# A decoder layer in split fp32 on one core: the weight ring moved by 32 bytes, GpSimd's additions given to VectorE, and two places for the modulation sums

## The chip, the core and the metric

The kernel runs on one core of a Trainium2 chip. A core has a matrix engine (TensorE, PE in the profile, with its weight loads as PEld), a vector engine (VectorE, DVE), a scalar engine (ScalarE, ACT), a general engine (GpSimd, POOL) and an engine that here only issues transfers (SyncE, SP). Each runs its own instructions in order. They share a memory on the chip of 128 partitions, in which addresses are counted in bytes of one partition. The metric is the time of one execution on the device in microseconds; lower is better.

## The reference

One layer of a decoder, 1024 tokens of width 1024, all in float32, cut to what is computed:

```python
mod = silu(cond) @ w_mod + b_mod
sh1, sc1, g1, sh2, sc2, g2, sh3, sc3, g3 = split(mod, 9)

h = rms_norm(x, ffn1_norm) * (1 + sc1) + sh1
x = x + 0.5 * g1 * ((silu(h @ w_gate1) * (h @ w_up1)) @ w_down1)      # FFN1, inner width 2816

h = rms_norm(x, mix_norm) * (1 + sc2) + sh2
b, c, v, u = split(h @ w_in, 4)                                       # each of width 512
yA = b * conv3_causal(c * v)
yB = gelu(Re(C . state) + D * u)       # state_t = Abar state_(t-1) + Bbar u_t, 32 groups of 64 states
yB = yB * sigmoid(yB @ glu_w + glu_b)
x = x + g2 * (concat(rms_norm(yA), rms_norm(yB)) @ w_out)

h = rms_norm(x, ffn2_norm) * (1 + sc3) + sh3
x = x + 0.5 * g3 * ((silu(h @ w_gate2) * (h @ w_up2)) @ w_down2)      # FFN2
return rms_norm(x, final_norm)
```

## The kernel before

**Stages.** In order of time: FFN1 (a prologue with the first norm, gate and up projections to 505 us, the down projection to about 720 us), the mixer's projections u, c, v and b with the eight batches of the state recurrence beside them, the GLU, the output projection `w_out` (about 985 to 1055 us), FFN2 (gate and up to about 1500 us, down to the end) and the last norm.

**Matmuls.** A float32 product is made of three passes (`mm3`, lines 324 to 326): the weight and the activation are each split into a high and a low part, and the passes are high by high, high by low and low by high, mostly with 128 weight columns and 512 moving columns. Both parts of a weight tile lie in one ring tile `w` of 8 KB a partition. ACT copies the high part into it (line 183), DVE subtracts it for the low part (line 184), from a raw tile of 8 KB that SP loads (`raw`). The ring has three buffers (`ringp`), a fourth in the middle of the kernel (`ring1b`), and, in the last down projection only, five more (`ring2`). A tile serves 24 matmuls of 512 columns in the feed-forward stages.

**Where the buffers lie.** Pools are stacked from the left or from the right end of a partition's memory. `ringp`, `rawp`, `tmp` (short-lived tiles) and `ring1b` stand on the right, above a block of constants whose last tile is a pad of `PAD[1]` columns of float32; `ring2`, the activations (`movA`) and others stand on the left, above a pad of `PAD[0]` columns. With 88 columns on the right the built program has the tiles of `ringp` at bytes 202720, 210912 and 219104 and that of `ring1b` at 165856, each 480 modulo 512. The five of `ring2` stand at 120320 to 153088, each 0 modulo 512.

**Feed-forward groups.** All but the first groups of gate and up, and both down projections, use seven products for eight (Strassen's scheme). It needs sums of weight blocks: `Weights.combine` (lines 151 to 153) makes them for gate and up from a raw tile, and `right_sums` (lines 602 to 605) for the down weights `wd`, which then go back to memory (line 612) until the down projection loads them. The sums of activations (`combos`, whose low parts line 336 makes, and `Left.sums`, lines 587 to 590) are DVE's.

**Who does what, and when.** A clock counts calls of `mm3`. Work can be put off by some ticks (`clock.after`), and generators in `clock.side` make one step every `clock.period` ticks. The tile framework then sets the order on each engine and the waits between engines. In FFN1 the weight sums run on DVE; in FFN2 `ws.adds` and an argument of `right_sums` put them on POOL. The sums of squares for the norms `n3` (before FFN2) and `n4` (the last) are accumulated by `Sumsq.add`: there `beside` sends the first five additions of each to POOL (line 353), the others run on DVE (line 355).

**Modulation.** Each of the nine modulation vectors takes eight sums over the condition (`mod_fetch`, line 447, loads 512 KB into a tile `wm`; `mod_next` multiplies and sums it on DVE, line 441). Those of G2, SC3 and SH3, 24 sums, are made by one generator `vectors` from the projection u on, one every 6 ticks. Beside them run the batches of the recurrence: a matmul group `px` (line 1297), a copy `X`, two transfers that swap halves (`swx`, `swz`, line 1287), products and scans on DVE (lines 1303 to 1314), and a matmul group `yy` (line 1324) that reads the result `co`. A loop behind the projections forces whatever of the sums is left (`while clock.side`).

The functions below also need these lines, which carry the last sums of squares of the mixer's norm: `roots` (lines 384 to 391) is a chain of twelve small DVE operations from the sums of squares to the reciprocal root.

Of the kernel before, what the change touches and what calls it, by code (L numbers as in the profile page):

```python
# [17 lines left out]
ALU = mybir.AluOpType  # L18
# [7 lines left out]
KT = D // P  # L26
# [17 lines left out]
GB = G // NB  # L44


PAD = 96, 88

C_BMOD, C_N1, C_N2, C_N3, C_NF, C_ONC, C_ONS, C_CW, C_GB = 0, 72, 80, 88, 96, 104, 108, 112, 124
NCOLS = 128  # L50
# [47 lines left out]
class Weights:  # L98
# [5 lines left out]
    SEVEN = (0, "t3", 1, 3, "t1", "t4", 2)  # L104

    def __init__(self, engines, srcs, granules, raw_bufs):
        self.V, self.A, self.SP, self.adds = engines
        self.srcs, self.granules, self.raw_bufs = srcs, granules, raw_bufs
        self.left = [0] * len(srcs)
        self.combined = {j for pair in granules for j, c in pair if isinstance(c, str)}  # L110
        for pair in granules:
            for j, _ in pair:
                self.left[j] += 1
        self.raws, self.tiles, self.sums, self.kinds = [], [], {}, []
        self.given = self.freed = 0
        self.sums_pool = None
        self.slots = deque()
# [27 lines left out]
    def combine(self, j):  # L145

        r = self.raws[j]
        t = self.sums_pool.tile([P, 3, HALF], F32, tag="sums", name=f"sums{j}")
        f = t[:].rearrange("p a b -> p (a b)")
        E = self.adds  # L150
        E.tensor_tensor(out=f[:, :1024], in0=r[:, 512:1536], in1=r[:, :1024], op=ALU.subtract)  # L151
        E.tensor_tensor(out=r[:, 512:1024], in0=f[:, 512:1024], in1=r[:, :512], op=ALU.add)
        E.tensor_tensor(out=f[:, 1024:], in0=r[:, 1536:], in1=r[:, 512:1024], op=ALU.subtract)
        self.sums[j] = {"t1": f[:, :512], "t3": f[:, 512:1024], "t4": f[:, 1024:]}

    def chunk(self, j, c):
# [55 lines left out]
def hymba_layer(ctx: ExitStack, tc, x_d, wm1_d, wmod_d, gu1_d, gs1_d, wd1_d, win_d, wout_d, glu_d, gu2_d, gs2_d, wd2_d, cols_d, cond_d, lam_d, bc_d, out_d):  # L212
    nc = tc.nc
    V, A, T, SP = nc.vector, nc.scalar, nc.tensor, nc.sync
# [4 lines left out]
    pad = pool("pad")  # L219
    pad.tile([P, PAD[0]], F32, name="pad_left")  # L220
    const = pool("const", side="right")
# [42 lines left out]
    srcs, granules = [], []  # L264
# [6 lines left out]
    t1_d, t2_d = (scratch.tile([4, KH, P, HALF], F32, name=f"t{n}_d")[:] for n in (1, 2))  # L271
# [25 lines left out]
    stream7(gu1_d, gs1_d, wd1_d, t1_d, SEVEN_FROM[0])  # L297
    plain([win_d[i] for i in range(8)] + [glu_d] + [wout_d[i] for i in range(4)])
    stream7(gu2_d, gs2_d, wd2_d, t2_d, SEVEN_FROM[1])
    ws = Weights((V, A, SP, V), srcs, granules, 2)  # L300
    ws.raw_pool = lambda i: rawp

    xt = [[None, None] for k in range(KT // 2)]
    x = [[None, None] for k in range(KT)]
# [8 lines left out]
    clock = Clock(4)  # L313
# [25 lines left out]
    class Sumsq:  # L339
# [3 lines left out]
            self.name, self.parts, self.n, self.home = name, [], n, home  # L343
            self.count = 0

        def add(self, src, apart=False, get=t2k, beside=False):
            nm, n = f"{self.name}q{self.count}", self.n
            sq = get(nm)[:] if self.parts else self.home(nm)
            A.activation(sq[:, :n], src, AF.Square)  # L349
            if self.parts and not apart:  # L350
                a = self.parts[0][:, :n]
                if beside:
                    nc.gpsimd.tensor_tensor(out=a, in0=a, in1=sq[:, :n], op=ALU.add)  # L353
                else:
                    V.tensor_tensor(out=a, in0=a, in1=sq[:, :n], op=ALU.add)
            else:
                self.parts.append(sq)
            self.count += 1
# [58 lines left out]
    def norm_into(act, h, ss, n, name, where="A", over=False):  # L417


        def use(bc):  # L420
            got = []
            for k in range(KT):
                clock.after(k, lambda k=k: got.append(modulated(k, h, bc, n, name, where, over)))
            act[h] = got

        ss.rstd(D, use, 8)
# [164 lines left out]
            self.store(2, 2, o[:])  # L591
            self.store(4, 2, e[:])

    def right_sums(k, wd_d, t_d, G_, where="A"):


        lo, hi = (mov(f"wd{k}_{i}", where, dtype=F32) for i in range(2))
        for i, t in enumerate((lo, hi)):
            SP.dma_start(t[:], wd_d[2 * i : 2 * i + 2, k].rearrange("c p n -> p c n"))
        b11, b12, b22, b21 = lo[:, 0, :], lo[:, 1, :], hi[:, 0, :], hi[:, 1, :]  # L600
        ops = [
            lambda: G_.tensor_tensor(out=b22, in0=b22, in1=b12, op=ALU.subtract),
            lambda: G_.tensor_tensor(out=b12, in0=b12, in1=b11, op=ALU.subtract),
            lambda: G_.tensor_tensor(out=b11, in0=b22, in1=b11, op=ALU.add),
            lambda: G_.tensor_tensor(out=b21, in0=b21, in1=b11, op=ALU.subtract),
        ]
        for i, op in enumerate(ops):
            clock.after(8 + 4 * i, op)

        def stores():  # L610
            for i, t in enumerate((lo, hi)):
                SP.dma_start(t_d[2 * i : 2 * i + 2, k].rearrange("c p n -> p c n"), t[:])

        clock.after(24, stores)
# [146 lines left out]
    for h in range(2):  # L761
        sqs = []
        for j in range(KT // 2):
            sq = pro.tile([P, 1024], F32, tag="sq", name=f"p{h}q{j}", bufs=3)
# [56 lines left out]
    left = Left(l1_d, 0, "fa0", "B")  # L821
# [287 lines left out]
    def vectors(count, where):  # L1109
        mod_fetch(where)  # L1110
        for i in range(count):
            mod_next()
            if i + 1 < count:
                mod_fetch(where)
            yield
# [41 lines left out]
    left = this  # L1157
    for g in range(SEVEN_FROM[0], NGRP):
        this = Left(l1_d, g, f"fa{g}", "B")
        hooks = {("g", 1): [left.sums], ("g", 5): [lambda g=g: right_sums(g - 2, wd1_d, t1_d, V, "B")]}  # L1160
        if g < 4:
            hooks["u", 5] = [lambda g=g: right_sums(g + 7, wd1_d, t1_d, V, "B")]
        if g == NGRP - 1:
            hooks["u", 2] = [lambda: lefts.load(2)]
            hooks["u", 5] = [lambda: lefts.load(4), lambda: lefts.ahead(3)]
        seven(f"fa{g}", this, hooks)
        left = this
# [67 lines left out]
    sp_open = ExitStack()  # L1235
    sp = sp_open.enter_context(tc.tile_pool(name="sp", bufs=1))
    clock.period = 6
    clock.side.append(vectors(3 * KT, "A"))
    w4 = ws.take(4)
    for h in range(2):  # L1240
        ready(act2, h, KT)
# [103 lines left out]
        ws.free()  # L1345
        v_tile(i, cs)

    while clock.side:
        clock.step()
    wb = ws.take(4)  # L1350

    def gate_b(i, h):
# [38 lines left out]
    n3 = [Sumsq(f"n3{c}", home=acc_in_mov) for c in "ab"]  # L1391
# [3 lines left out]
    def w_out(ds, h, part):  # L1395

        act = (actA, actB)[part]
        if part == 0:
            outs.update({(d, h): ps(f"wo{d}_{h}") for d in ds})
        for k in range(4):  # L1400
            ready(act, h, k + 1)
            for d in ds:
                mm3(outs[d, h][:], wo[d], 4 * part + k, act[h][k], part == k == 0, part == 1 and k == 3)
        if part == 0:
            return
        for d in ds:
            V.scalar_tensor_tensor(
                out=x[d][h], in0=outs.pop((d, h))[:], scalar=gate[:, 1, d : d + 1], in1=x[d][h], op0=ALU.mult, op1=ALU.add
            )
            n3[h].add(x[d][h], beside=d < 6)  # L1410
            if d % 2:
                SP.dma_start(x2_d[h, :, d - 1 : d + 1, :], xt[d // 2][h][:])

# [3 lines left out]
    w_out((0, 1), 0, 0)  # L1417
    glu(1)
    ws.free(2)
    wo.update(enumerate(ws.take(2), 2))  # L1420
    w_out((0, 1), 1, 0)
    w_out((0, 1), 0, 1)
# [10 lines left out]
    wo.update(enumerate(ws.take(4), 4))  # L1433
    w_out((4, 5, 6, 7), 0, 0)
    w_out((4, 5, 6, 7), 0, 1)
    norm_into(act3, 0, n3[0], 2, "h3", "B", True)
    ws.retire(ring1)
    for ds in ((4, 5), (6, 7)):
# [30 lines left out]
        ws.free()  # L1469
        return left  # L1470

    ws.adds = nc.gpsimd
    clock.period = 3
    clock.side.append(combos(act3, 2, "h3"))
    left = group0()
    lefts = Lefts(l2_d, "fbL")
    for g in range(1, NGRP):
        this = Left(l2_d, g, f"fb{g}")

        if 2 <= g:  # L1480
            mod_fetch("B")
            clock.after(40, lambda: fetched and mod_next())
        hooks = {("g", 1): [left.sums, lambda g=g: right_sums(g, wd2_d, t2_d, nc.gpsimd)]}
        if g == 4:
            hooks["u", 5] = [lambda: right_sums(0, wd2_d, t2_d, nc.gpsimd)]
        if g == NGRP - 1:
            hooks["g", 1].append(lambda: lefts.load(2))
            hooks["u", 5] = [lambda: lefts.load(4), lambda: lefts.ahead(3)]
        seven(f"fb{g}", this, hooks)
        left = this  # L1490
# [17 lines left out]
    def after2(d, h, done):  # L1508
        for tok in PIECES[h] if done == slice(0, HALF) else [done]:
            n = tok.stop - tok.start  # L1510
            if (h, tok.start) not in n4:
                n4[h, tok.start] = Sumsq(f"n4_{h}_{tok.start}", n, acc_in_mov)
            ss = n4[h, tok.start]
            ss.add(x[d][h][:, tok], apart=ss.count == KT - 1, beside=ss.count < 6)

            def use(bc, n=n, tok=tok):
                for k in range(KT):
                    xs = x[k][h][:, tok]
                    V.scalar_tensor_tensor(out=xs, in0=xs, scalar=cols[:, C_NF + k : C_NF + k + 1], in1=bc[:, :n], op0=ALU.mult, op1=ALU.mult)
                    if k % 2:  # L1520
                        SP.dma_start(out_d[h, :, k - 1 : k + 1, tok], xt[k // 2][h][:, :, tok])

            if ss.count == KT:
                ss.rstd(D, use)
# [70 lines left out]
```

## Time and profile before

| | |
|---|---|
| median of 3 runs | 1744.43 us (1743.91 to 1744.8) |
| the profiled execution | 1744.45 us, of which the span is 1742.5 |
| mean granted clock of TensorE | 0.992 |
| PE busy | 1685.0 us (97%), 7496 matmuls |
| DVE busy | 1212.8 us (70%) |
| ACT busy | 627.8 us (36%) |
| POOL busy | 217.1 us (12%), 135 instructions |

A page of the profile shows one execution. An engine's busy time is what its instructions took. "Idle before" is the time in which it stood, and the arrow names what ended that. In a list of instructions `w<-raw,w` means that tile `w` is written from `raw` and `w`; the numbers of tiles are left out. The table by stage cuts the span at times that I chose from where the tiles of a stage begin, and gives each engine's busy time within. Most of what follows is read from that table, from the list of who waited for whom, and from the instructions in order of time.

### The profile page before, as it was taken

The page shows a single profiled execution, that of the slowest core. Times are in us where ns is not written, and L with a number is a line of the kernel's source. Part 1 is how long each engine was busy: PE and PEld are TensorE (multiplying, and loading weights), DVE is VectorE, ACT ScalarE, POOL GpSimd, SP SyncE. Part 2 cuts the span into 40 slices and gives each one's busy share as a digit, 9 for nine tenths or more (in the row PEclk, how much of TensorE's full clock was granted, in tenths as well). Part 3 has the DMA queues.
Part 4 walks back from the last instruction along what each step waited for, and adds up shares of the span by engine and source line. Part 5 has one row for each costly group of instructions (what it writes and reads, how often), then busy time and mean ns, then how long its engine had stood idle before and what let it go on. Part 6 is the DMA issues. An engine that isn't in the chain of part 4 may idle for free.

```text
span 1742.5 us, 20320 instructions
## 1 busy us (share of the span) xinstructions
PE 1685.0 (97%) x7496; PEld 1358.3 (78%) x7496; DVE 1212.8 (70%) x2068; ACT 627.8 (36%) x957; POOL 217.1 (12%) x135
## 2 busy tenths in 40 slices
PE   4999999999999999999999999989999999999997
PEld 3788777777777888877888877867888888888887
DVE  7999876777778976847757639866566655557464
ACT  4333333333343434421115324523333333435340
POOL 0000000000000000000000021245453444101020
PEclk9999999999999999999999999999999999999998
DMA  7325765555588884668752211454443444667532
GB/s 304 122 71 176 246 233 191 177 183 170 170 297 295 312 297 163 220 196 261 224 151 67 73 73 51 138 199 167 179 167 145 163 162 174 242 237 257 209 126 97
DMA packets 149685, 321.81 MB, mean 185 GB/s; under 512 B 19793, under 2 KB 35409, under 8 KB 141266
## 3 DMA queue, kind: packets, MB, share of 16 engines
q1 hardware_dynamic: 149586, 320.53, 53.6%
q8 instruction: 58, 0.95, 0.2%
q14 instruction: 41, 0.34, 0.1%
HBM read 229.77 MB, written 86.51 MB: 182 GB/s over the span
## 4 chain that ended last, share of the span: by engine, by line
PE 85%; DVE 8%; DMA 4%; issue 1%; POOL 1%; ACT 1%; SPq 0%; DVEq 0%; ACTq 0%; POOLq 0%
PE fbDX L326 2%; PE fbDX L324 2%; PE fbDX L325 2%; PE faDX L324 2%; PE faDX L326 2%; PE faDX L325 2%; PE faDY L325 2%; PE faDY L326 2%; PE faDY L324 2%; PE fbDY L326 2%; PE fbDY L325 2%; PE fbDY L324 2%; PE wo L326 1%; PE wo L325 1%; PE wo L324 1%; DMA wm<-in_wmod 1%
## 5 line engine op out<-in xcount | busy, mean ns | idle before, releaser
L184 DVE TENSOR_TENSOR w<-raw,w 128x512 fp32r<-128x512 f32 (+1 forms) x268 | 267.2, 1003 | 157.5 <-ACT w L183 156.8
L183 ACT CAST w<-raw 128x512 fp32r<-128x512 f32 (+1 forms) x268 | 211.3, 803 | 291.0 <-PE faDX L326 59.4
L184 DVE TENSOR_TENSOR w<-sums,w 128x512 fp32r<-128x512 f32 x114 | 86.2, 770 | 85.3 <-ACT w L183 85.3
L353 POOL TENSOR_TENSOR n3aq<-n3aq,n3aq 128x512 f32<-128x512 f32 x5 | 6.5, 1291 | 1005.7 <-ACT n3aq L349 1005.5
L183 ACT CAST w<-sums 128x512 fp32r<-128x512 f32 x114 | 68.8, 620 | 77.4 <-POOL sums L151 4.7
L441 DVE CUSTOM_DVE_ANT_0 wm<-wm,cact 128x1024 f32<-128x1024 f32 x56 | 69.0, 1239 | 33.6 <-DMA wm<-in_wmod 33.4
L151 POOL TENSOR_TENSOR sums<-raw 128x1024 f32<-128x1024 f32 x20 | 54.8, 2739 | 192.9 <-DVE w L184 185.5
L326 PE MATMUL fbDX<-fbLh,w 128*128 128x512 f32 (+1 forms) x220 | 77.9, 354 | 0.0
L324 PE MATMUL fbDX<-fbLh,w 128*128 128x512 f32 (+1 forms) x220 | 77.8, 354 | 0.0
L325 PE MATMUL fbDX<-fbLl,w 128*128 128x512 f32 (+1 forms) x220 | 77.7, 353 | 0.0
L324 PE MATMUL faDX<-faLh,w 128*128 128x512 f32 x176 | 70.2, 403 | 2.1 <-ACT faLh L638 2.1
L325 PE MATMUL faDX<-faLl,w 128*128 128x512 f32 x176 | 70.0, 398 | 0.0
L326 PE MATMUL faDX<-faLh,w 128*128 128x512 f32 x176 | 69.9, 397 | 0.0
L639 DVE TENSOR_TENSOR fbLl<-fbLr,fbLh 128x1024 fp32r<-128x1024 f32 (+1 forms) x42 | 48.9, 1173 | 13.3 <-ACT fbLh L638 11.7
L325 PE MATMUL faDY<-faLl,w 128*128 128x512 f32 x132 | 52.2, 396 | 0.5 <-DVE faLl L639 0.5
L326 PE MATMUL faDY<-faLh,w 128*128 128x512 f32 x132 | 52.1, 395 | 0.0
L326 PE MATMUL fbDY<-fbLh,w 128*128 128x512 f32 x132 | 51.8, 393 | 0.0
L324 PE MATMUL fbDY<-fbLh,w 128*128 128x512 f32 x132 | 51.8, 393 | 0.0
L325 PE MATMUL fbDY<-fbLl,w 128*128 128x512 f32 x132 | 51.8, 393 | 0.0
L324 PE MATMUL faDY<-faLh,w 128*128 128x512 f32 x132 | 51.7, 395 | 0.0
L639 DVE TENSOR_TENSOR faLl<-faLr,faLh 128x1024 fp32r<-128x1024 f32 (+1 forms) x42 | 47.2, 1128 | 4.0 <-ACT faLh L638 4.0
L325 PEld LDWEIGHTS fbDX<-fbLl,w 128*128 128x128 f32 x220 | 42.5, 193 | 6.0
(2133 smaller groups left out, 4748.9 us busy)
## 6 DMA issues: line engine op xcount, KB each, us to landing
raw<-in_gs SPq DMA_DIRECT2D x38, 1024.0 KB, 5.5
wm<-in_wmod SPq DMA_DIRECT2D x56, 512.0 KB, 6.5
wd<-in_wd SPq DMA_DIRECT2D x44, 512.0 KB, 5.2
t_d<-wd SPq DMA_DIRECT2D x44, 512.0 KB, 3.5
faLr<-l_d SPq DMA_DIRECT2D x35, 512.0 KB, 8.1
fbLr<-l_d SPq DMA_DIRECT2D x35, 512.0 KB, 6.6
raw<-t_d SPq DMA_DIRECT2D x16, 1024.0 KB, 5.6
raw<-in_wd SPq DMA_DIRECT2D x12, 1024.0 KB, 5.6
```

Source lines behind the costliest of these rows:

```text
L151: E.tensor_tensor(out=f[:, :1024], in0=r[:, 512:1536], in1=r[:, :1024], op=ALU.subtract)
L183: self.A.copy(hi, src)
L184: self.V.tensor_tensor(out=lo, in0=src, in1=hi.bitcast(F32), op=ALU.subtract)
L324: T.matmul(out, lhsT=hi, rhs=ah, start=first, stop=False, skip_group_check=more)
L325: T.matmul(out, lhsT=hi, rhs=al, start=False, stop=False, skip_group_check=more)
L326: T.matmul(out, lhsT=lo, rhs=ah, start=False, stop=last, skip_group_check=more)
L353: nc.gpsimd.tensor_tensor(out=a, in0=a, in1=sq[:, :n], op=ALU.add)
L441: V.tensor_tensor_reduce(out=w, in0=w, in1=cact[:], scale=1.0, scalar=0.0, op0=ALU.mult, op1=ALU.add, accum_out=s)
L639: V.tensor_tensor(out=lo[:, :c, :], in0=src, in1=hi[:, :c, :].bitcast(F32), op=ALU.subtract)
```

## The change

Three edits:

1. `PAD` goes from `96, 88` to `96, 80`: the right-hand pad is eight columns (32 bytes) shorter, and all that stands to its left on that side moves by 32 bytes. In the built program `ringp`'s tiles then begin at 202752, 210944 and 219136 and `ring1b`'s at 165888, all 0 modulo 512; the raw tiles and the short-lived ones move in the same way. The left-hand pools stay.
2. POOL keeps only the set-up of constants. Its 129 additions go to DVE: the weight sums of FFN2's gate and up (20 sets of three), FFN2's right sums (44), and the ten additions of `n3` and fifteen of `n4`.
3. Of the 24 modulation sums, the eight of G2 stay where they were, and the sixteen of SC3 and SH3 are made from behind the second half of the GLU on, one every 4 ticks; the loop that forces the rest stands behind the output projection's first half for columns 4 to 7, ahead of the norm that uses them.

```diff
-PAD = 96, 88
+PAD = 96, 80
...
-        self.V, self.A, self.SP, self.adds = engines
+        self.V, self.A, self.SP = engines
...
-        E = self.adds
-        E.tensor_tensor(out=f[:, :1024], in0=r[:, 512:1536], in1=r[:, :1024], op=ALU.subtract)
-        E.tensor_tensor(out=r[:, 512:1024], in0=f[:, 512:1024], in1=r[:, :512], op=ALU.add)
-        E.tensor_tensor(out=f[:, 1024:], in0=r[:, 1536:], in1=r[:, 512:1024], op=ALU.subtract)
+        self.V.tensor_tensor(out=f[:, :1024], in0=r[:, 512:1536], in1=r[:, :1024], op=ALU.subtract)
+        self.V.tensor_tensor(out=r[:, 512:1024], in0=f[:, 512:1024], in1=r[:, :512], op=ALU.add)
+        self.V.tensor_tensor(out=f[:, 1024:], in0=r[:, 1536:], in1=r[:, 512:1024], op=ALU.subtract)
...
-                if beside:
-                    nc.gpsimd.tensor_tensor(out=a, in0=a, in1=sq[:, :n], op=ALU.add)
-                else:
-                    V.tensor_tensor(out=a, in0=a, in1=sq[:, :n], op=ALU.add)
+                V.tensor_tensor(out=a, in0=a, in1=sq[:, :n], op=ALU.add)
...
-            lambda: G_.tensor_tensor(out=b22, in0=b22, in1=b12, op=ALU.subtract),
+            lambda: V.tensor_tensor(out=b22, in0=b22, in1=b12, op=ALU.subtract),
...
     clock.period = 6
-    clock.side.append(vectors(3 * KT, "A"))
+    clock.side.append(vectors(KT, "A"))
...
         v_tile(i, cs)
 
-    while clock.side:
-        clock.step()
     wb = ws.take(4)
...
-            n3[h].add(x[d][h], beside=d < 6)
+            n3[h].add(x[d][h])
...
     w_out((0, 1), 0, 0)
     glu(1)
     ws.free(2)
+    clock.period = 4
+    clock.side.append(vectors(2 * KT, "A"))
     wo.update(enumerate(ws.take(2), 2))
...
     w_out((4, 5, 6, 7), 0, 0)
     w_out((4, 5, 6, 7), 0, 1)
+    while clock.side:
+        clock.step()
     norm_into(act3, 0, n3[0], 2, "h3", "B", True)
...
-    ws.adds = nc.gpsimd
     clock.period = 3
...
-        hooks = {("g", 1): [left.sums, lambda g=g: right_sums(g, wd2_d, t2_d, nc.gpsimd)]}
+        hooks = {("g", 1): [left.sums, lambda g=g: right_sums(g, wd2_d, t2_d)]}
```

Three places show how the instructions stand on DVE. In the rows a line number comes first, then the operation, output and inputs and the shape. Since the change takes a few lines out, a line of the changed kernel has a number lower by one to six.

The first place is the mixer, from the scans of the first batch to its result `co` (the tile read by the first `yy`). `wm` rows are the modulation sums (each with a short row that reads out the accumulator), `ya` and `cs` the convolution. Before:

```order
L1308 SCALAR_TENSOR_TENSOR sz_6396<-r_585,X_6394 128x128 x4
L432 TENSOR_TENSOR scl<-ms_6241,cols 128x8
L1311 TENSOR_TENSOR si_6318<-sz_6396,si_6318 128x512
L1313 TENSOR_TENSOR co_6316<-sz_6396,co_6316 128x512
L435 SCALAR_TENSOR_TENSOR scl<-scl,cols 128x8
L1253 TENSOR_TENSOR cs_6326<-cs_6326,v_1_6447 128x512
L441 ISA wm_0_6452,ms_6535<-wm_0_6452,cact 128x1024
L441 ISA ms_6535 128x1
L184 TENSOR_TENSOR w_6508<-raw_6215,w_6508 128x1024
L1259 TENSOR_SCALAR ya_5942<-cs_6326,cols 128x1024
L441 ISA wm_1_6475,ms_6535<-wm_1_6475,cact 128x1024
...
L1314 TENSOR_TENSOR co_6316<-co_6316,swz_6409 128x512
```

The same place in the changed kernel:

```order
L1304 SCALAR_TENSOR_TENSOR sz_6378<-r_585,X_6376 128x128 x4
L1307 TENSOR_TENSOR si_6309<-sz_6378,si_6309 128x512
L1309 TENSOR_TENSOR co_6307<-sz_6378,co_6307 128x512
L1249 TENSOR_TENSOR cs_6317<-cs_6317,v_1_6426 128x512
L1310 TENSOR_TENSOR co_6307<-co_6307,swz_6391 128x512
```

The modulation sums no longer stand between the scans and `co`, and two other operations that stood there come later.

The second place is the output projection, around the root `nBb` of the second norm of yB's halves (lines 384 to 391 before) and the split of a weight tile ahead of it. `y` rows (line 1407) evacuate a finished product. Before:

```order
L184 TENSOR_TENSOR w_7849<-raw_7475,w_7849 128x1024
L384 TENSOR_SCALAR nBbnv<-nBbst 128x4
L385 TENSOR_SCALAR nBbni<-nBbnv 128x4
L386 TENSOR_SCALAR nBbni<-nBbni 128x4
L389 TENSOR_TENSOR nBbna<-nBbni 128x4
L390 SCALAR_TENSOR_TENSOR nBbna<-nBbna,nBbnv 128x4
```

The same place in the changed kernel:

```order
L183 TENSOR_TENSOR w_7796<-raw_7422,w_7796 128x1024
L437 ISA wm_1_7812,ms_7814<-wm_1_7812,cact 128x1024
L437 ISA ms_7814 128x1
L437 ISA wm_2_7816,ms_7814<-wm_2_7816,cact 128x1024
...
L380 TENSOR_SCALAR nBbnv<-nBbst 128x4
L381 TENSOR_SCALAR nBbni<-nBbnv 128x4
L437 ISA wm_3_7831,ms_7814<-wm_3_7831,cact 128x1024
...
L385 TENSOR_TENSOR nBbna<-nBbni 128x4
```

Two modulation sums stand ahead of the root, one within it.

The third place is FFN2's head, from a weight split of its second group to the second one after. `wd` rows are the right sums. Before (the right sums and the weight sums are on POOL):

```order
L184 TENSOR_TENSOR w_8929<-raw_8620,w_8929 128x512
L184 TENSOR_TENSOR w_8929<-sums_8838,w_8929 128x512
L441 ISA wm_2_9354,ms_9273<-wm_2_9354,cact 128x1024
L441 ISA ms_9273 128x1
L184 TENSOR_TENSOR w_8966<-sums_8838,w_8966 128x512
L184 TENSOR_TENSOR w_8966<-raw_8620,w_8966 128x512
```

The same place in the changed kernel:

```order
L183 TENSOR_TENSOR w_8929<-raw_8620,w_8929 128x512
L183 TENSOR_TENSOR w_8929<-sums_8838,w_8929 128x512
L598 TENSOR_TENSOR wd_1_8860<-wd_1_8860,wd_0_8859 128x512
L599 TENSOR_TENSOR wd_0_8859<-wd_0_8859 128x512
L600 TENSOR_TENSOR wd_0_8859<-wd_1_8860,wd_0_8859 128x512
L437 ISA wm_2_9354,ms_9273<-wm_2_9354,cact 128x1024
L437 ISA ms_9273 128x1
L601 TENSOR_TENSOR wd_1_8860<-wd_1_8860,wd_0_8859 128x512
L183 TENSOR_TENSOR w_8966<-sums_8838,w_8966 128x512
L183 TENSOR_TENSOR w_8966<-raw_8620,w_8966 128x512
```

The four right sums stand between the two splits, around the modulation sum.

More of the change, by code (lines that the diff above doesn't have):

```diff
@@ L299, in hymba_layer @@
     stream7(gu2_d, gs2_d, wd2_d, t2_d, SEVEN_FROM[1])
-    ws = Weights((V, A, SP, V), srcs, granules, 2)
+    ws = Weights((V, A, SP), srcs, granules, 2)
     ws.raw_pool = lambda i: rawp
@@ L344, in __init__, with add @@
             self.count = 0
-        def add(self, src, apart=False, get=t2k, beside=False):
+        def add(self, src, apart=False, get=t2k):
             nm, n = f"{self.name}q{self.count}", self.n
@@ L592, in sums, with right_sums @@
             self.store(4, 2, e[:])
-    def right_sums(k, wd_d, t_d, G_, where="A"):
+    def right_sums(k, wd_d, t_d, where="A"):
         lo, hi = (mov(f"wd{k}_{i}", where, dtype=F32) for i in range(2))
@@ L601, in right_sums @@
         ops = [
[L602 to L605, printed above, removed]
+            lambda: V.tensor_tensor(out=b22, in0=b22, in1=b12, op=ALU.subtract),
+            lambda: V.tensor_tensor(out=b12, in0=b12, in1=b11, op=ALU.subtract),
+            lambda: V.tensor_tensor(out=b11, in0=b22, in1=b11, op=ALU.add),
+            lambda: V.tensor_tensor(out=b21, in0=b21, in1=b11, op=ALU.subtract),
         ]
@@ L1159, in hymba_layer @@
         this = Left(l1_d, g, f"fa{g}", "B")
-        hooks = {("g", 1): [left.sums], ("g", 5): [lambda g=g: right_sums(g - 2, wd1_d, t1_d, V, "B")]}
+        hooks = {("g", 1): [left.sums], ("g", 5): [lambda g=g: right_sums(g - 2, wd1_d, t1_d, "B")]}
         if g < 4:
-            hooks["u", 5] = [lambda g=g: right_sums(g + 7, wd1_d, t1_d, V, "B")]
+            hooks["u", 5] = [lambda g=g: right_sums(g + 7, wd1_d, t1_d, "B")]
         if g == NGRP - 1:
@@ L1482, in hymba_layer @@
             clock.after(40, lambda: fetched and mod_next())
-        hooks = {("g", 1): [left.sums, lambda g=g: right_sums(g, wd2_d, t2_d, nc.gpsimd)]}
+        hooks = {("g", 1): [left.sums, lambda g=g: right_sums(g, wd2_d, t2_d)]}
         if g == 4:
-            hooks["u", 5] = [lambda: right_sums(0, wd2_d, t2_d, nc.gpsimd)]
+            hooks["u", 5] = [lambda: right_sums(0, wd2_d, t2_d)]
         if g == NGRP - 1:
@@ L1513, in after2 @@
             ss = n4[h, tok.start]
-            ss.add(x[d][h][:, tok], apart=ss.count == KT - 1, beside=ss.count < 6)
+            ss.add(x[d][h][:, tok], apart=ss.count == KT - 1)
             def use(bc, n=n, tok=tok):
```

## The prediction

> **What bounds the kernel now.** I read the busy times first, then the chain that ended last, then the busy time by stage.
>
> ```profile
> PE 1685.0 (97%) x7496; PEld 1358.3 (78%) x7496; DVE 1212.8 (70%) x2068; ACT 627.8 (36%) x957; POOL 217.1 (12%) x135
> PE 85%; DVE 8%; DMA 4%; issue 1%; POOL 1%; ACT 1%; SPq 0%; DVEq 0%; ACTq 0%; POOLq 0%
> 0.00:65.00 65.00, 39.31 (x140) 29.50 (x141) 52.02 (x102) 24.82 (x30) 0.70 (x6) 1.00 0.67 260
> 65.00:205.00 140.00, 140.00 (x602) 112.44 (x601) 132.07 (x449) 52.10 (x91) 0.00 (x0) 1.00 0.44 142
> 205.00:505.00 300.00, 300.00 (x1321) 236.19 (x1320) 224.60 (x381) 116.53 (x203) 0.00 (x0) 1.00 0.61 198
> 755.00:880.00 125.00, 117.00 (x571) 96.45 (x570) 76.49 (x128) 24.51 (x35) 0.00 (x0) 0.99 0.76 235
> 985.00:1050.00 65.00, 64.36 (x285) 51.62 (x284) 26.08 (x42) 15.17 (x22) 13.89 (x9) 1.00 0.21 81
> 1050.00:1180.00 130.00, 121.68 (x519) 96.47 (x518) 102.75 (x144) 52.91 (x89) 36.61 (x21) 0.98 0.38 131
> 1180.00:1480.00 300.00, 300.00 (x1285) 240.97 (x1284) 177.60 (x201) 109.50 (x198) 138.66 (x81) 1.00 0.45 164
> ```
>
> In the stage rows the columns are length, then PE, PEld, DVE, ACT and POOL busy, then clock and DMA. TensorE sets the time: 97% busy, 85% of the chain, and busy 300.00 of 300 us in both long feed-forward stages. So two things can be gained: a matmul that starts sooner after the one before it, and the 57.5 us (1742.5 less 1685.0) in which PE is idle, 25.7 of them in the first 65 us, 8.0 in the mixer's middle stage (755 to 880) and 8.3 at the head of FFN2 (1050 to 1180). A free GpSimd is worth nothing by itself.
>
> **The ring, 32 bytes lower: the large term.** The matmuls of before already run with weights at both alignments. In the program's allocation the right-hand rings hold their tiles at 480 modulo 512, and the five buffers of `ring2`, which the last down projection mixes in, stand at 0. Each weight tile feeds 24 matmuls of 512 columns. I cut the stretches at the starts of whole tiles, and counted only matmuls that read a `w` tile.
>
> ```profile
> 541.70:547.30 5.60, 5.60 (x26) 1.00 1.03 393
> 1584.71:1590.16 5.45, 5.45 (x25) 1.00 0.58 212
> 1590.16:1606.95 16.79, 16.79 (x73) 1.00 0.88 308
> 1651.11:1667.43 16.32, 16.32 (x73) 1.00 0.41 146
> 0.00:1742.50 1742.50, 1626.97 (x6996) 0.99 0.54 185
> 1690.00:1742.50 52.50, 34.11 (x262) 0.86 0.21 81
> ```
>
> The columns are length, PE busy (and rows that touch the stretch, so one or two more than it holds), clock, DMA share and rate. Three tiles at 480 take 16.79 us for 72 matmuls, 233.2 ns each; three at 0 take 16.32 us, 226.7 ns each, at the same clock, in the same stage, with the same moving operands' pools. One tile at 0 alone (1584.71) takes 5.45 us, and it stands between tiles at 480. The difference is 6.5 ns a matmul. All rows outside the tail are 6996 less 262, or 6734; ten tiles of 24 already stand at 0, which leaves 6494 matmuls, times 6.5 ns 42.2 us. That holds if every one of them follows its predecessor without a wait. In the tail the matmuls have 256 columns and I count nothing there.
>
> Where PE does not set the pace the term shrinks. In the first 65 us PE is idle for 25.7 us, DVE busy for 52; I strike its part (104 of such matmuls, 0.7 us). From 65 to 205 us DVE is busy 132.07 of 140, and the 602 matmuls would shorten PE by 3.9 us to 136: DVE still fits, barely; I strike 1.3 us. I enter **−40 us**; its bounds are −34 (if another 6 us are lost at waits of DVE) and −42.
>
> Is it the address modulo 512, or merely another place in memory? The first row is a tile in `ring1b`, which the allocation puts at byte 165856, 480 modulo 512, right above `ring2`, whose buffers reach up to 161280. It takes 5.60 us, as the tiles of `ringp` do at 202720 and above. A limit by place would have to lie in the 4.5 KB between. I hold the alignment for the cause, at nine in ten.
>
> [...]
>
> **GpSimd's 129 additions to DVE.** Outside FFN2's head and the tail the cover is PE's lead.
>
> ```profile
> L151 POOL TENSOR_TENSOR sums<-raw 128x1024 f32<-128x1024 f32 x20 | 54.8, 2739 | 192.9 <-DVE w L184 185.5 <-DVE y L412 7.3
> L151 DVE TENSOR_TENSOR sums<-raw 128x1024 f32<-128x1024 f32 x13 | 15.8, 1217 | 0.0
> L153 DVE TENSOR_TENSOR sums<-raw 128x512 f32<-128x512 f32 x13 | 8.9, 687 | 0.2
> L184 DVE TENSOR_TENSOR w<-raw,w 128x512 fp32r<-128x512 f32 x61 | 60.8, 1007 | 45.8 <-ACT w L183 45.7
> L184 DVE TENSOR_TENSOR w<-raw,w 128x512 fp32r<-128x512 f32 x55 | 37.0, 682 | 0.2
> L184 DVE TENSOR_TENSOR w<-sums,w 128x512 fp32r<-128x512 f32 x46 | 38.3, 847 | 52.5 <-ACT w L183 52.5
> L590 DVE TENSOR_TENSOR fb4s<-fb4l,fb4s 128x512 f32<-128x512 f32 x1 | 2.8, 2775 | 0.0
> L554 DVE TENSOR_TENSOR fb6gc<-fb6ge,fb6gc 128x512 f32<-128x512 f32 x1 | 1.8, 1780 | 0.0
> ```
>
> An addition of 1024 costs DVE 1217 ns, one of 512 687, against 2739 and some 1300 to 1700 on POOL. From 1180 to 1480 the 81 operations of POOL (138.66 us) cost DVE about 14 times 1.217 plus 67 times 0.687, or 63 us. But beside POOL, DVE itself is slower: the split of 512 (L184) takes 1007 ns in that stage (x61) and 682 in the FFN1 stage 205 to 505 where POOL is still (x55), 20 us over 61; the 46 splits of sums take 847 instead of 687 ns, 7 us; eight L590 like the one shown lose 2.1 us each, 17; six L554 lose 1.1 each, 6. Some 50 us come back. So DVE's 177.60 becomes about 191 of 300, less than the 224.60 with which FFN1 runs the same work at PE 300.00 of 300. I enter **0**, between −0 (PE has nothing left to gain there) and +10 (a wait in every group).
>
> **FFN2's head, 1050 to 1180.** Here PE is idle for 8.32 us.
>
> ```profile
> PE fb2uB L324 <- ACT fb2uB L542: 4.3, 1, 4.3
> PE fb0g L325 <- DVE h L414: 1.5, 2, 0.7
> PE fb2gC L326 <- DVE w L184: 1.5, 1, 1.5
> DVE wm L441 <- DMA wm<-in_wmod: 21.5, 5, 6.6
> SPq L612 <- POOL wd L604: 25.4, 2, 14.1
> 1107.85 6.91 DVE L336 TENSOR_TENSOR h3S<-y,h3S 128x512 fp32r<-128x512 f32 x4
> 1129.37 1.30 POOL L602 TENSOR_TENSOR wd<-wd,wd 128x512 f32<-128x512 f32 x1 [15.15 <-DMA wd<-in_wd]
> ```
>
> Two things on DVE's way are POOL's doing. Four splits beside POOL's sums take 6.91 us, the four before them 2.49. The right sums run on POOL from 1129.37 to 1136.3; SP's stores wait for them, the next `wm` fetches stand behind those stores, and DVE, in order, waits 21.5 us for `wm` with PE's weight splits queued behind. On DVE the four sums need 2.7 us instead of 6.9, so the stores and the fetches behind them go some 4 us earlier. Against it DVE now meets `wd` itself: it reaches the row after its split at 1124.8 and the load lands at 1129.37, 4.6 us of waiting, about what it now spends waiting for `wm` at that row (to 1130.46). I enter **−5**; bounds −8.3 (all the idle time) and +4 (the 4.6 us in the path at w146).
>
> **The modulation sums out of the mixer's chain.** From 755 to 880 PE idles for 8.0 us.
>
> ```profile
> PE yy L1324 <- DVE co L1314: 4.8, 2, 3.1
> PE px L1297 <- DMA ub<-u_d: 3.2, 2, 2.3
> 792.18 1.14 DVE wm L441
> 796.62 1.13 DVE wm L441
> 799.56 1.13 DVE wm L441
> 831.40 1.21 DVE wm L441
> ```
>
> Three `wm` sums, 3.40 us, stand in the chain to the first `yy`, which is 3.1 late; one, 1.21, stands ahead of the second, 1.7 late. Taken away, they return 3.1 and 1.2; of the 3.2 at `px`, where SP has fewer fetches ahead of `ub`, I count 0.9. Sum **−5**, bounds −2 and −8.
>
> **The same sixteen sums in the output projection.** Here DVE is busy for 26.08 of 65 us, and sixteen at 1.22 add 19.5: there is room.
>
> ```profile
> PE wo L326 <- DVE w L184: 0.6, 1, 0.6
> wm<-in_wmod SPq DMA_DIRECT2D x56, 512.0 KB, 6.5
> ```
>
> What hurts is order, not load: a sum whose 512 KB have not landed (6.5 us from issue) blocks the splits and norm steps behind it. Three sums now stand before and among the steps of the `nBb` root, and three more ahead of the splits of w134 and w135, the last of which is 0.6 us late already. I enter **+2** (two sums at 1.22 less what little slack there is); bounds 0 and +6.5, one whole landing.
>
> **The tail.**
>
> ```profile
> PE n_0st L364 <- DVE n_0q L355: 1.4, 1, 1.4
> 1689.23 2.67 POOL L353 TENSOR_TENSOR n_0q<-n_0q,n_0q 128x512 f32<-128x512 f32 x2 [20.45 <-ACT n_0q L349]
> ```
>
> Two additions on DVE take 1.4 instead of 2.67 us, and PE waits 1.4 for them: **−1**, bounds −1.4 and +1.
>
> **The sum.** −40 + 0 − 5 − 5 + 2 − 1 = −49. The profiled execution took 1744.45 us (1742.5 of span and 1.95 around it), which is the median, 1744.43, to 0.02. Forecast **1695 us**.
>
> **The rivals.**
>
> 1. *The spacing depends on the place, not on the alignment, or on nothing that 32 bytes change.* For it: the two kinds of ring lie in different parts of memory. Against it: the 5.60 us in the low ring buffer. Then only −9 is left: about 1735 us. 8%.
> 2. *DVE becomes the bound where PE gets faster.* From 65 to 205 it is already at 94%, and it takes over additions of some 96 us (44 right sums at 0.687, twenty sets at 2.59, the squares). The first loses 4 us, and a wait of 1 us in each of ten FFN2 groups 10 more: about 1710 us. Against it: FFN1's 224.60 of 300 without a stall of PE. 17%.
> 3. *Slower: the right sums block DVE.* In each FFN2 group DVE, in order, waits for `wd`, queued on SP behind stores that themselves wait; the splits of the next weight tiles stand behind it. POOL's wait of 15.15 us shows how late a load can be. If PE has one weight tile in hand, 5.45 us, up to 9.7 us may be lost in each of ten groups: 97 − 49 is +48, about 1792 us; it decides the sign when a group loses more than 4.9 us. Against it: that wait was POOL's, idle and early; the load itself lands in about 5 us after its issue and DVE's rows stand behind splits of later tiles. 4%.
> 4. *The idle times close wholly*: −42, −8.3, −8 and −1.4 with nothing paid, 1685 us. 6%.
>
> **How the numbers follow.** The forecast's case has 65%; the bounds of its terms, which will hardly all fall on one side, give about 1688 to 1704. To leave out no more than two in ten I reach to the second rival's 1710 and a little beyond, and down to the fourth: **1684 to 1714**, which leaves out the first, the third and a part of the second. A measurement of this kernel tells 0.2%, 3.5 us, from no change. Faster takes all cases but the third, and 3 of 100 for the first together with waits: 0.93; the same 0.02; slower 0.05.
>
> **What would show it.** Whole tiles of 24 matmuls at about 5.44 us everywhere show the first term; 5.60 refutes it. DVE's split of 512 at about 0.69 us in 1180 to 1480 shows the end of the contention, and PE busy in the whole of that stage shows that the additions are covered; waits of PE for L184's line, with DVE waiting for `wd`, would be rivals 2 and 3. No wait of PE for `co` shows the mixer's term, and a wait for a split in the output projection its price. The forecast is wrong if the ring's spacing stays, or if PE's idle time grows above 57.5 us.

## The result, and the profile after

The changed kernel takes 1686.99 us (median of 4 runs, 1685.72 to 1689.79) against 1744.17 for the one before: a ratio of 0.9681, with a 95% interval of 0.9658 to 0.9705, so 51 to 60 us less. The forecast of 1695 us had the direction and most of the size; the time lies near the lower end of the range given.

The engines' busy times and the chain that ended last, of the changed kernel:

```profile
PE 1639.3 (97%) x7496; PEld 1356.5 (80%) x7496; DVE 1227.4 (73%) x2197; ACT 628.8 (37%) x957; POOL 0.7 (0%) x6
PE 91%; DVE 5%; DMA 2%; ACT 1%; issue 1%; SPq 0%; DVEq 0%; ACTq 0%
```

PE does the same 7496 matmuls in 45.7 us less, and its idle time falls from 57.5 to 46.5 us (1685.8 of span less 1639.3). DVE has taken over all of POOL's additions and its busy time has grown by only 14.6 us.

Stretches of PE with only the matmuls that read a ring tile (length, busy and rows that touch it, clock, DMA share, rate), of the changed kernel; the first is the three tiles of `ring2` shown before, the second the tile in `ring1b`:

```profile
1598.61:1614.93 16.32, 16.32 (x73) 1.00 0.42 152
533.80:539.24 5.44, 5.44 (x25) 1.00 1.02 366
```

The tile in `ring1b` now takes 5.44 us for its 24 matmuls instead of 5.60, like those of `ring2`.

DVE's groups in FFN2's steady part of the changed kernel, and the busy time of all engines there (PE, PEld, DVE, ACT, POOL):

```profile
L183 DVE TENSOR_TENSOR w<-raw,w 128x512 fp32r<-128x512 f32 x61 | 41.3, 687 | 16.9 <-ACT w L182 16.7
...
L150 DVE TENSOR_TENSOR sums<-raw 128x1024 f32<-128x1024 f32 x14 | 17.0, 1218 | 0.0
```

```profile
1158.00:1453.00 295.00, 295.00 (x1304) 244.33 (x1303) 183.89 (x274) 113.66 (x203) 0.00 (x0) 1.00 0.48 173
```

The split of 512 is back from 1007 to 687 ns; DVE is busy for 184 of 295 us with POOL's work included, and PE never stops. The waits of PE that are new, or left over from those the prediction spoke of, in the changed kernel:

```profile
PE fa3uB L323 <- ACT fa3uB L538: 2.8, 1, 2.8
...
PE wo L325 <- DVE w L183: 1.8, 1, 1.8
PE px L1293 <- DMA ub<-u_d: 1.3, 1, 1.3
```

No wait for `co` in the mixer, none for `fb2uB` or a split at FFN2's head, none for `n_0q` in the tail. In their place stand a wait at 190 us in FFN1 that was not there before, and a longer one in the output projection.

**Where the time went.** Cut at the first matmul of a ring tile (w14, w30 and so on; the same work in each kernel), the stages of the profiled executions took, in us:

| stage, by ring tiles | before | after | ring alone | additions alone | sums alone |
|---|---|---|---|---|---|
| start to w14 (prologue, first groups) | 164.1 | 160.8 | 160.7 | 164.2 | 163.9 |
| w14 to w30 (FFN1, DVE nearly full) | 93.3 | 95.6 | 95.2 | 93.3 | 93.3 |
| w30 to w71 (FFN1) | 240.4 | 234.2 | 234.2 | 240.4 | 240.3 |
| w71 to w114 (FFN1 down, u) | 268.7 | 261.8 | 262.1 | 267.6 | 269.2 |
| w114 to w122 (mixer, c and v) | 118.0 | 106.6 | 116.6 | 116.6 | 108.6 |
| w122 to w132 (b, GLU) | 123.8 | 121.1 | 121.0 | 123.8 | 124.4 |
| w132 to w136 (output projection) | 47.6 | 49.3 | 46.5 | 46.7 | 49.5 |
| w136 to w152 (FFN2's head) | 125.7 | 112.2 | 124.3 | 115.2 | 124.6 |
| w152 to w243 (FFN2, down) | 508.0 | 495.2 | 495.2 | 508.0 | 508.0 |
| w243 to the end | 53.0 | 49.1 | 51.6 | 48.7 | 51.4 |
| span | 1742.5 | 1685.8 | 1707.3 | 1724.6 | 1733.3 |

The last three columns are the first three experiments that follow. A column is one execution; that of the ring alone, 1709.13 us, is the slowest of its four. Each part gains where it was expected to, and two stages lose.

### The profile page after: what moved, and what is told of

Same layout as the page of the kernel before. It is cut to its first block, busy times and chain, and to the rows that moved or that the text cites. A ratio compares the mean times of both kernels' runs of the same rounds, so it can differ in the third digit from the quotient of the medians.

```text
span 1685.8 us, 20261 instructions
## 1 busy us (share of the span) xinstructions
PE 1639.3 (97%) x7496; PEld 1356.5 (80%) x7496; DVE 1227.4 (73%) x2197; ACT 628.8 (37%) x957; POOL 0.7 (0%) x6
## 4 chain that ended last, share of the span: by engine, by line
PE 91%; DVE 5%; DMA 2%; ACT 1%; issue 1%; SPq 0%; DVEq 0%; ACTq 0%
PE faDX L324 2%; PE faDX L323 2%; PE faDX L325 2%; PE fbDX L325 2%; PE fbDX L323 2%; PE fbDX L324 2%; PE faDY L324 2%; PE fbDY L325 2%; PE fbDY L323 2%; PE fbDY L324 2%; PE faDY L325 2%; PE faDY L323 2%; PE wo L325 2%; PE wo L323 2%; PE wo L324 2%; DVE mw L437 1%
## 5 line engine op out<-in xcount | busy, mean ns | idle before, releaser
L183 DVE TENSOR_TENSOR w<-raw,w 128x512 fp32r<-128x512 f32 (+1 forms) x268 | 243.0, 913 | 120.5 <-ACT w L182 119.9
L183 DVE TENSOR_TENSOR w<-sums,w 128x512 fp32r<-128x512 f32 x114 | 76.6, 686 | 64.9 <-ACT w L182 64.7
L635 DVE TENSOR_TENSOR fbLl<-fbLr,fbLh 128x1024 fp32r<-128x1024 f32 (+1 forms) x42 | 47.2, 1131 | 11.0 <-ACT fbLh L634 10.7
L325 PE MATMUL faDY<-faLh,w 128*128 128x512 f32 x132 | 51.4, 389 | 0.0
L634 ACT CAST faLh<-faLr 128x1024 fp32r<-128x1024 f32 (+1 forms) x42 | 40.8, 977 | 21.0 <-DMA faLr<-l_d 21.0
L150 DVE TENSOR_TENSOR sums<-raw 128x1024 f32<-128x1024 f32 x38 | 46.3, 1218 | 0.0
```

Of the source, the lines that this page charges most:

```text
L150: self.V.tensor_tensor(out=f[:, :1024], in0=r[:, 512:1536], in1=r[:, :1024], op=ALU.subtract)
L183: self.V.tensor_tensor(out=lo, in0=src, in1=hi.bitcast(F32), op=ALU.subtract)
L325: T.matmul(out, lhsT=lo, rhs=ah, start=False, stop=last, skip_group_check=more)
L634: A.copy(hi[:, :c, :], src)
L635: V.tensor_tensor(out=lo[:, :c, :], in0=src, in1=hi[:, :c, :].bitcast(F32), op=ALU.subtract)
```

## The experiments

### Each part by itself

The ring alone, on the kernel before:

```diff
-PAD = 96, 88
+PAD = 96, 80
```

> The kernel before with the right-hand pad at 80 columns, and nothing else: the ring at 0 modulo 512. My theory (each of the 6494 matmuls of 512 columns starts 6.5 ns sooner, and PE sets the pace almost everywhere): whole tiles of 24 matmuls at 5.44 us, and 41 us off, about 1703 us. Rival (the spacing is bound to be 6.5 ns shorter, but DVE, still slowed by GpSimd, becomes the bound in FFN2): PE idle inside 1180 to 1480 and less than 35 us off, above 1709.

Measured: 1703.56 us, ratio 0.9775 (0.9751 to 0.9799), 40.5 us less by the medians. Three ring tiles of FFN2's down projection take 16.32 us, as those of `ring2` do:

```profile
1557.81:1574.13 16.32, 16.32 (x73) 1.00 0.83 290
```

The first theory holds. The rival does not: from w152 to w243 this kernel needs 495.2 us, as the full change does, with POOL still at work beside DVE. DVE's relief was not needed for the faster matmuls.

The additions alone (`V` in place of `ws.adds`, `G_` and `nc.gpsimd`, as in the change; pad and sums as before):

> The kernel before with GpSimd's 129 additions on DVE, and nothing else. By the stage times of the changed kernel this part is worth about 10 us in FFN2's head and 4 in the tail, beyond the shorter spacing: 1731 us, with no wait of PE for ACT at fb2uB. Rival, that DVE's waits for wd cost what the relief brings: 1740 to 1748, with a new wait of PE for splits between 1050 and 1480.

Measured: 1727.69 us, ratio 0.9911 (0.9892 to 0.9929), 16 us less by the medians. FFN2's head gains 10.5 us and the end 4.3; from w152 to w243, where 93 operations of POOL moved to DVE, it is 508.0 us as before. All that is left of PE's waits between 1050 and 1180 us:

```profile
PE n3bbc L400 <- DVE n3brb L394: 1.1, 1, 1.1
```

The rival falls: no wait for a split, none for ACT.

The sums alone (`vectors(KT)` in the u stage, `vectors(2 * KT)` behind the second half of the GLU, the forcing loop moved; pad and POOL as before):

> The kernel before with the modulation sums of SC3 and SH3 moved to the output projection, and nothing else. Theory: the sums in DVE's chain made PE wait for co and ub, so 8 to 9 us come off between 755 and 880, and 3 are lost in the output projection: 1739 us. Rival, that the mixer was relieved by the faster matmuls or by luck of the transfers: the waits for co stay, and the time is 1744 or above.

Measured: 1736.94 us, ratio 0.9966 (0.9945 to 0.9987), 7.2 us less by the medians. From w114 to w122 it takes 108.6 instead of 118.0 us; what PE waits for between 755 and 880 us is one transfer:

```profile
PE px L1297 <- DMA ub<-u_d: 0.9, 1, 0.9
```

The output projection gives back 1.9 us. The theory holds, the rival falls.

All but the ring, on the changed kernel:

```diff
-PAD = 96, 80
+PAD = 96, 88
```

> The changed kernel with the right-hand pad back at 88 columns: additions on DVE and the moved modulation sums, the ring at 480 modulo 512. If the parts add, the changed kernel's 1687 plus 42, about 1729 us, with tiles of 24 at 5.60 us. If DVE's relief is worth more where PE is slow, or the parts hide one another, it lies more than 4 us beside that.

Measured: 1722.02 us, ratio 0.9874 (0.9855 to 0.9893). Three tiles take 16.79 us again:

```profile
1568.66:1585.45 16.79, 16.79 (x74) 1.00 0.85 300
```

It is 7 us faster than the parts would add up to. In the profiled execution (1718.51 us, the fastest of the four) two stages account for that: this kernel takes 93.3 us from w14 to w30 and 47.1 in the output projection, where the full change, with 2.5 and 1.2 us less to be expected from the spacing, takes 95.6 and 49.3. In the first, the faster matmuls bring PE to a place before DVE is done. In the second this execution was lucky: other runs with the slow spacing wait there as well ("The two new waits" has them).

### Is it the ring's address, or its relation to something else?

The prediction laid the spacing to the weights' address modulo 512. These runs move one side or the other. The edits are to the one line, on the changed kernel:

```diff
-PAD = 96, 80
+PAD = 96, 64    # first run: ring at 64 modulo 512
+PAD = 96, 72    # second run: ring at 32
+PAD = 88, 80    # third run: activations and ring2 at 480, ring at 0
```

> The changed kernel with the right-hand pad at 64 columns: the ring at 64 modulo 512. Theory A (a multiple of 64 bytes is enough): tiles of 24 matmuls at 5.44 us, as in the changed kernel, 1687 us. Theory B (it has to be a multiple of 512, the length of one row of 128 weights): 5.60 us and about 1722 us.

> The changed kernel with the right-hand pad at 72 columns: the ring at 32 modulo 512, in other places than before but 32 off a multiple of 64 again. Both alignment theories: 5.60 us for 24 matmuls, about 1722 us. If the place decided, not the alignment, the tiles would be somewhere else than 5.60.

> The changed kernel with the left-hand pad at 88 columns: all left-hand pools 32 bytes lower, so that the activations and the five buffers of ring2 stand at 480 modulo 512 and the right-hand ring stays at 0. If only the weights' address counts and not the place: ten tiles in ring2 at 5.60 us, the others of the last down projection at 5.44, and 1.6 us more in all, 1689 us. If the place counts: ring2 stays at 5.44. If the moving operand's address counts as the weights' does: all tiles at 5.60 or more, 1722 us or above.

Measured, one run each: 1722.83, 1722.87 and 1722.83 us. Three ring tiles of the same down projection with the ring at 64, then at 32:

```profile
1572.12:1588.91 16.79, 16.79 (x73) 1.00 0.83 299
```

```profile
1572.76:1589.55 16.79, 16.79 (x73) 1.00 0.83 299
```

Both are slow, so a multiple of 64 bytes is not enough. The third run is the one that counts. The first row is three ring tiles at 0, the second three tiles of `ring2` at 480, both with activations at 480:

```profile
1572.26:1589.05 16.79, 16.79 (x73) 1.00 0.83 299
...
1633.23:1649.56 16.33, 16.33 (x74) 1.00 0.44 160
```

The weights at a multiple of 512 are now the slow ones, and those at 480 the fast. That refutes what the prediction held for the cause, at nine in ten: the weights' own address does not decide. Place does not either, since `ring1b` is slow or fast with the pads. What the fast cases have in common is that weights and moving operand lie at the same place modulo 512. Nor are the raw and short-lived tiles, which move with the right-hand pad, the cause: the tiles of `ring2`, filled from the same raw tiles, are fast in all three runs (226.8 to 227.3 ns a matmul). A new theory, then, and three runs for it:

```diff
-PAD = 96, 80
+PAD = 88, 88    # first run: both at 480
+PAD = 96, 16    # second run: ring at 256, activations at 0
+PAD = 96, 48    # third run: ring at 128, activations at 0
```

> The changed kernel with both pads at 88 columns: ring and activations both at 480 modulo 512. New theory (a matmul starts 6.5 ns later when its weights and its moving operand lie at different places modulo 512, whatever the places are): 5.44 us for 24 matmuls everywhere, 1687 us. Old theory (the weights must lie at a multiple of 512): 5.60 us, 1722 us.

> The changed kernel with the right-hand pad at 16 columns: the ring at 256 modulo 512, the activations at 0. If the two addresses have to agree modulo 512: 5.60 us for 24 matmuls, 1722 us. If modulo 256 is enough: 5.44 us, 1687 us.

> The changed kernel with the right-hand pad at 48 columns: the ring at 128 modulo 512, the activations at 0. If the two addresses have to agree modulo 128 only: 5.44 us for 24 matmuls, 1687 us; if modulo 256 or 512: 5.60 us, 1722 us.

Measured, one run each: 1686.55, 1685.61 and 1714.34 us. Three ring tiles each, both at 480 first, then 256 against 0, then 128 against 0:

```profile
1537.84:1554.16 16.32, 16.32 (x73) 1.00 0.81 284
```

```profile
1537.46:1553.78 16.32, 16.32 (x73) 1.00 0.85 303
```

```profile
1564.44:1581.19 16.75, 16.75 (x73) 1.00 0.82 303
```

With both sides at 480, off any multiple of 64, the kernel is as fast as the change. A difference of 256 costs nothing; one of 128 costs nearly all (232.6 ns a matmul by the mean, against 233.3 at 32 and 64, and 226.9 when they agree). So it is the difference of the two addresses, modulo 256, over the six differences tried (0, 32, 64, 128, 256 and 480). Of the 8.5 us between that run's 1714 and the 1723 of the three before, the 0.7 ns less for each of 6494 matmuls are 4.5, and a wait in the output projection that it happened to have only for 0.4 us another 1.5 to 3.3 (47.2 us there, against 48.7 to 50.5).

One more, for a difference below 32 bytes:

```diff
-PAD = 96, 80
+PAD = 96, 76
```

> The changed kernel with the right-hand pad at 76 columns: the ring at 16 modulo 512, the activations at 0. If the two addresses must agree modulo 256: 5.60 us for 24 matmuls, 1722 us. If an offset smaller than 32 bytes costs nothing or less: 5.44 us and 1687 us, or between.

Measured: 1687.69 us and 16.31 us for three tiles. It answers nothing: the allocator rounded the pad of 304 bytes up to 320, so the ring stood at 0 in the built program, and the run repeats the changed kernel. Differences below 32 bytes were not tried.

### The two new waits

The wait in FFN1, by DVE's instructions in order of time (changed kernel): `bb` needs the parameters `prm` of the recurrence, whose load SP issues at 180.04 us. The row names a store, `t_d<-wd`, which SP issues right behind it; in the kernel before, the same wait is put down to the load of `prm`.

```profile
183.55 0.68 DVE L550 TENSOR_TENSOR fa3gc<-fa3ge,fa3gc 128x512 f32<-128x512 f32 x1
189.91 0.22 DVE L1023 TENSOR_TENSOR bb<-prm,qr 128x64 f32<-128x64 f32 x1 [5.68 <-DMA t_d<-wd]
```

DVE stands for 5.68 us with the weight splits and the evacuation of `fa3ge` behind it. In the kernel before, it stood there for 4.7 us and PE did not wait; nor did PE in any run with the slow spacing but one, while it did in all with the fast one until the edit below. The wait in the output projection (same view): the last split of w135 stands behind two modulation sums whose loads are late.

```profile
982.60 1.23 DVE L437 CUSTOM_DVE_ANT_0 wm<-wm,cact 128x1024 f32<-128x1024 f32 x1 [0.53 <-DMA wm<-in_wmod]
...
985.29 1.23 DVE L437 CUSTOM_DVE_ANT_0 wm<-wm,cact 128x1024 f32<-128x1024 f32 x1 [1.45 <-DMA wm<-in_wmod]
...
987.04 1.22 DVE L183 TENSOR_TENSOR w<-raw,w 128x1024 fp32r<-128x1024 f32 x1
```

This wait does not hang on the spacing. With the ring at 64, then at 32 (2.0 also with the left-hand pad moved), PE waits for the same split:

```profile
PE wo L325 <- DVE w L183: 1.8, 1, 1.8
...
PE wo L325 <- DVE w L183: 2.0, 1, 2.0
```

The run with all but the ring and the one at 128 waited 0.2 and 0.4 us there, so with the slow spacing it comes and goes; all four runs profiled with the fast spacing and sums every 4 ticks, the changed kernel among them, waited 1.8 to 2.2.

The edit takes both on:

```diff
-        if g < 4:
-            hooks["u", 5] = [lambda g=g: right_sums(g + 7, wd1_d, t1_d, "B")]
+        if 5 <= g < 7:
+            hooks["u", 5] = [lambda g=g: right_sums(g + 4, wd1_d, t1_d, "B")]
...
-    clock.period = 4
+    clock.period = 5
     clock.side.append(vectors(2 * KT, "A"))
```

> The changed kernel with two edits, told apart by stage: the sixteen modulation sums in the output projection at every 5 ticks instead of 4, and the two right sums that FFN1's groups 2 and 3 make besides their own made in groups 5 and 6 instead. If the stall in the output projection (1.8 us of waiting for the last split of w135 and 1.6 more at half clock) comes from the sums queued ahead of that split: gone, 3 us off between 980 and 1030. If the stall at 190 us (2.8 and 1.6) comes from DVE, which is full there and stands 5.7 us for a load: 3 to 4.4 us off before 256 us. Both: 1680 us. Rival: the load of prm is as late as before and the wait only moves: 1684.

Measured: 1681.18 us (1680.37 to 1682.48), ratio 0.9642 (0.9612 to 0.9672). From w14 to w30 it takes 91.1 instead of 95.6 us, in the output projection 46.6 instead of 49.3, and of the wait for the split 0.3 us is left:

```profile
PE wo L325 <- DVE w L183: 0.3, 1, 0.3
```

Both waits are gone with the edit. For the output projection that speaks for the queued sums. In FFN1 the cause is less sharply shown: DVE now stands 0.5 us for `bb` instead of 5.7, but the edit took four additions of DVE and their loads and stores out of those groups at once, so which of the two counted is not shown. This kernel beats the one before by 62 us, and its four runs all lie below those of the changed kernel, with their intervals against the kernel before still touching.

## Why the prediction was right, and where it was wrong

- **The ring, −40.** Right in size: −40.5 alone, and matmuls at 226.9 ns as read from the ten tiles in `ring2`. The count of 6494 and the 6.5 ns held in every stage without a wait: 12.8 us from w152 to w243, 6.2 from w30 to w71. The wait that the faster matmuls bring in FFN1 is contained in the 40.5. Wrong in its cause: the step "I hold the alignment for the cause, at nine in ten" took the weights' address for what decides. Before, all moving operands stood at 0 modulo 512, so the rows of that trace could not tell the weights' address from its difference to theirs. With the activations 32 bytes off, the ring of the changed kernel is slow again, as the run with the left-hand pad moved shows.
- **What DVE takes from it, 1.3 from 65 to 205 us.** Too little. The strike assumed that DVE, with 132 us of work, would just fit into the 136 that PE would need; what counted was not how busy it was but one transfer, for which it stood 5.7 us with splits queued behind. From w14 to w30, where that happens, 2.3 us were lost where the spacing alone would have brought 2.5.
- **The additions, 0 in steady FFN2.** Right: 508.0 us with and without. The estimate of DVE's busy time there (191 of 300) came out at 184 of 295.
- **FFN2's head, −5 with a bound of −8.3, and the tail, −1.** Right in the mechanism, and mis-sized: −10.5 and −4.3 in the run with the additions alone, beyond both bounds. The bound took PE's idle time for the whole price of a wait. After some waits PE ran at half clock (0.50 in the first row below), which the page counts as busy. Shown are, in the kernel before, the stretch behind the 4.3 us at `fb2uB` and the beginning of the tail; then the beginning of the tail with the sums alone, which leaves the additions on POOL, and in the changed kernel (columns as in the stage rows, the clock third from the end):

```profile
1177.00:1181.20 4.20, 4.20 (x11) 3.26 (x10) 2.96 (x5) 0.86 (x2) 3.29 (x2) 0.50 0.79 267
...
1689.50:1700.00 10.50, 9.15 (x52) 8.92 (x51) 4.08 (x17) 1.60 (x3) 2.32 (x2) 0.68 0.01 2
```

```profile
1681.90:1692.40 10.50, 9.18 (x65) 8.95 (x64) 4.74 (x18) 2.03 (x4) 3.03 (x3) 0.84 0.01 2
```

```profile
1636.70:1647.00 10.30, 10.22 (x86) 9.99 (x85) 6.86 (x22) 1.94 (x4) 0.00 (x0) 1.00 0.01 2
```

  Ten matmuls at 427 instead of 233 ns cost 2 us more; in the tail 86 matmuls go where 52 went. Part of that gain is luck, namely of the execution that stands for the kernel before: behind the same wait the sums alone ran that stretch at clock 0.84 instead of 0.68 and took 51.4 us for the tail, not 53.0, so the additions are worth 2.7 to 4.3 us there.
- **The mixer, −5, bounds −2 and −8.** Right in the mechanism, as the waits for `co` went with the sums, and too small: 9.4 us alone (118.0 to 108.6; the run with the additions alone, with the sums in place, took 116.6). The 8.0 us of idle time were again not the whole price: behind the wait of 3.1 us at the first `yy`, too, four matmuls start 427 ns apart, at a clock of 0.50 from 802.47 to 805.88 us.
- **The output projection, +2.** The sums alone cost 1.9 us; with the fast ring it is 3.0 more than the spacing alone would give (49.3 against the 46.3 that 47.6 becomes with 6.5 ns less for 192 matmuls). In the five runs with all but the fast spacing the stage took 47.1 to 50.5 us, so the price lay between nothing and 3 us as the loads landed. The mechanism, a sum that stands for its load in front of the last split, is the one named.
- **The rivals.** DVE did not become the bound in FFN2, and no group lost time to `wd`: DVE waited for it, 10.6 us in five places, within PE's lead. The second rival was right only in FFN1, for some 4.5 us (95.6 against 91.1 without the wait).

The sum of the parts run alone is larger than the whole: 40.5, 16.4 and 7.2 are 64, and the change gives 57. In the profiled executions it is 62.3 against 56.7. There 3.4 of the 5.6 us lie in the tail, where the kernel before ran slowest and each part alone shows a shorter time, and 1.8 in the output projection. The new wait in FFN1 is no part of it, since the ring alone has it too (95.2 us from w14 to w30). The medians carry a few us of uncertainty each, so no more is to be read from the difference.

## What to carry to other kernels

Where a trace holds the same matmul at two paces, cut the stretches at whole tiles and compare the addresses of all operands, not of the one that differs: here it was the difference between weights and moving operand that had to be a multiple of 256 bytes, as far as the differences tried show. Price a wait of the matrix engine by its length and by the clock of the few microseconds behind it (0.50 for 3.4 us behind two waits of the changed kernel). After a gain on the bounding engine, look for the places where another engine stood for a load unseen; two small edits at such places were worth another 6 us.

## What the runs showed of the hardware

**The addresses of weights and moving operand.** In these runs the fp32r matmuls with 512 moving columns took 226.9 ns each by the mean when the addresses of weights and moving operand differed by 0 or 256 modulo 512 (16.32 us for 72), and 232.6 to 233.3 when they differed by 32, 64, 128 or 480 (16.75 to 16.79 us for 72). The weight loads' own durations in the trace were 187 to 188 ns by the median, before and after the change. With 256 columns, in the last stage, nothing was gained: the median from start to start was 120 ns in the kernel before and in the changed one. The runs do not show why the difference matters.

**Half clock behind a wait.** Two waits of the changed kernel and the stretches behind them (PE busy, then the other engines, the clock third from the end):

```profile
190.60:193.70 3.10, 0.28 (x2) 0.00 (x0) 3.10 (x7) 1.65 (x4) 0.00 (x0) 1.00 0.94 365
...
194.50:197.90 3.40, 3.40 (x9) 2.63 (x8) 3.33 (x6) 0.70 (x2) 0.00 (x0) 0.50 0.26 95
986.10:988.30 2.20, 0.39 (x2) 0.00 (x0) 2.20 (x5) 0.00 (x0) 0.00 (x0) 1.00 0.59 181
989.80:992.80 3.00, 3.00 (x8) 2.32 (x7) 1.66 (x6) 0.00 (x0) 0.00 (x0) 0.50 0.85 306
```

The slow stretch begins 0.8 and 1.5 us after work has resumed, and lasts 3.4 us: eight matmuls at 427 ns, 1.6 us more than at full clock. It does not follow every wait. In the kernel before, 2.67 us between two matmul starts at 777 us were followed by none (clock 1.00 from 780 to 797 us), while the second stretch above came behind 2.21 us. The 2.47 us between two matmul starts at the beginning of FFN1's down projection were followed by one in both kernels (clock 0.51 from 522.5 to 526.0 us before, and from 515.3 to 518.8 us in the changed one). So the length of the wait alone does not decide it here; what does is not shown.
